# A hybrid decoder trunk on one core: fixed bank for seventeen accumulators, fused value products, one scaling on GpSimd, and two norms' factors through DRAM

## The chip, the cores and the metric

The kernel runs on one core of one Trainium2 chip. The metric is the device time of one execution in microseconds. Before the change it is 1033.41 us, the median of three runs (1032.59 to 1033.46).

A core has engines that run side by side: TensorE (PE: matrix products; its weight loads are listed as PEld), VectorE (DVE), ScalarE (ACT), GpSimd (POOL) and SyncE (SP, which here only issues transfers). Each takes its own instructions in order and waits on semaphores of the others. TensorE writes its sums to eight banks of PSUM, each 128 partitions by 512 float32; a bank is free for the next sum when DVE or ACT has read it.

## The reference, cut to what matters

Two layers over 512 tokens of 1024 channels, in float32. The first is a Conformer convolution module and a SwiGLU feed-forward part. The second takes queries, attends over keys and values that are projected once, and has its own feed-forward part:

```python
def rmsnorm(x, g):
    xf = x.astype(jnp.float32)
    xf = xf * lax.rsqrt(jnp.mean(xf * xf, axis=-1, keepdims=True) + EPS)
    return (xf * g.astype(jnp.float32)).astype(x.dtype)
...
            if l == N_A_LAYERS:
                kv = rmsnorm(h, norm_kv) @ w_kv
                k_flat, v_flat = jnp.split(kv, 2, axis=-1)
...
            q = (rmsnorm(h, norm_mix[l]) @ w_q[j]).reshape(B, S, N_HEADS, HEAD_DIM)
            attn = banded_sink_attention(q, k_shared, v_shared, sinks[j], rel_bias)
            h = h + attn @ w_o[j]
        h = h + swiglu_ffn(rmsnorm(h, norm_ffn[l]), ffn_w_up[l], ffn_w_down[l])
    return rmsnorm(h, norm_final)
```

Keys and values have four heads of 64 channels each, so the value projection is a product of 512 tokens by 1024 channels by 256 columns.

## The kernel before, in words

The activations stay in SBUF with channels on the partitions and the 512 tokens along the free axis. Weights come as 258 chunks of 512 KB (128 partitions by 1024 floats) in the order of `PLAN`; SyncE's queue loads them into six `raw` buffers, nine chunks ahead at most (`load`, L286). Most chunks are then split into a rounded high part `whi` (ACT, L322) and the rest `wlo` (DVE, L325), four buffers of each, since a float32 product is made of three products of parts, high by high, high by low and low by high (`mm3`, L418 to L420). Sums of weight blocks that the seven-product scheme of the feed-forward parts needs are prepared in DRAM: SyncE copies a block (L300), GpSimd's queue adds another to it (L314), and a later load reads it.

An RMS norm's factor is one number for each token. `Rms.add` squares and adds the channels' tiles; `step1` sums over the partitions with matmuls into four columns (L533), makes mean and epsilon on DVE (L535) and the power of -1/2 on GpSimd (L538), so that `rs` holds the factors with tokens on the partitions. To multiply tiles that have tokens along the free axis, the factors must stand in every partition: DVE puts them on the diagonals of four blocks (`diag`, L543; for two blocks it is ACT, L548), a matmul with a matrix of ones spreads them into a bank (`spread`, L562), and ACT copies this to `bc` (L556). The norm is not multiplied into the inputs of the products but into their results, so `bc` is read only when a product is evacuated. Two norms have all four blocks (n == 4): the one of keys, values and queries, whose `step1` and `step2` stand around the projection of the values, and the one of the second feed-forward part.

The keys come first (`kb`, 24 matmuls of 512 columns for each of two halves of the channels). Then the values (`vb`, four banks, one for each 128 tokens): there the tokens are the stationary operand, and for each of 8 channel blocks and 4 token blocks `mm3` streams 256 columns of `whi`, of `wlo` and of `whi` again. DVE scales them to `vq` (L1499). `query(0, 0)` follows, then a change of the PSUM pools: the pool of eight banks (`ps8`) is closed, and a pool of one (`ps1`) and one of seven (`ps7`) are opened in its place, since the later stages keep one bank apart (`last_bank`). Then `query(0, 1)` and the attention run as a pipeline, whose score tiles `sc` (four buffers of 128 by 4 by 257 floats) lie in a pool that was opened before the last down projection of the first layer.

The order within each engine is that of a planner in the language's framework, which simulates the program and places what is ready; `issue_after` in the code holds some instructions behind others. It also chooses which bank of a pool an accumulator gets.

At the end the last product comes in four blocks of 128 tokens and two halves g of the channels. For each block the sum of squares, its power (`power`, GpSimd) and the scaling (`scale`) follow, then the store. `then` keeps the order of these steps on each engine as written. `ends` is the last block, number 3; half 0 of a block is scaled by ACT, half 1 by DVE, and SyncE's queue stores all pieces but one, which goes by ACT's queue.

Of the kernel before, what the change touches and what calls it, by code (L numbers as in the profile page):

```python
# [18 lines left out]
P = 128  # L19
# [26 lines left out]
SEVEN = ("A11 B11", "S1 T1", "S2 T2", "A12 B21", "S3 T3", "S4 B22", "A22 T4")  # L46
LOWS = ((0, 2, 4), (6, 8))
# [170 lines left out]
def hybrid_trunk(ctx: ExitStack, tc: tile.TileContext, xT, W, prm_in, wdw_in, sinks, relb, onehot, fin, lead, out):  # L218
# [14 lines left out]
    room, stay = ExitStack(), ExitStack()  # L233
    ctx.enter_context(room)
    ctx.enter_context(stay)
    psum_at = [room.enter_context(tc.tile_pool(name="ps8", bufs=8, space=PSUM))]
    last_bank, rooms, spare, turn, alone = [], [], [], [0], [0]
# [4 lines left out]
    def bank():  # L242
        if spare:
            spare.append(spare.pop(0))
            return rooms[spare[-1]][:, 0].rearrange("p a s -> p (a s)") if spare[-1] is not None else one_of(last_bank[0])
        turn[0] = (turn[0] + alone[0]) % 8
        return one_of(last_bank[0] if turn[0] == 7 else psum_at[0])
# [85 lines left out]

    def advance():
        u = stream["use"]
        share[1] += share[0]
        for _ in range(2):
            if share[1] >= 1 and not withheld:
                share[1] -= 1
                next(preparing[0], None)  # L340
        load(u + DMA_AHEAD)
        while stream["split"] < min(len(PLAN), u + SPLIT_AHEAD):
            i = stream["split"]
            stream["split"] += 1
            if i in NATIVE:
                splits[i] = (raws.pop(i), None)
                continue
            hi = wpool.tile([P, 1024], F32R, tag="whi", name=uid("whi"))
            lo = wpool.tile([P, 1024], F32R, tag="wlo", name=uid("wlo"))
            splits[i] = (hi, lo)  # L350
            split_weights(hi, lo, raws.pop(i))
# [46 lines left out]
    def get(*key):  # L398
# [11 lines left out]
        return tuple(w and w.rearrange("p (a b) -> p a b", **sh) for w in (hi, lo))  # L410

# [96 lines left out]
    class Rms:  # L508
# [17 lines left out]
        def step1(self):  # L526
# [12 lines left out]
            if self.pinned:  # L539
                biased[0] = mean  # L540
            self.diag = temp()[:, 0:self.w]
            if n == 4:
                nc.vector.tensor_mul(self.diag.rearrange("p (n q) -> p n q", n=n),  # L543
                                     ident.unsqueeze(1).to_broadcast([P, n, P]),
                                     self.rs.unsqueeze(2).to_broadcast([P, n, P]))
            else:
                for i in range(n):
                    self.turned = nc.scalar.mul(self.diag[:, i * P:(i + 1) * P], ident, self.rs[:, i:i + 1]).ins  # L548
# [855 lines left out]

    part2 = ExitStack()
# [57 lines left out]
    if True:  # L1463
# [19 lines left out]
        for half in range(2):  # L1483
            whi, wlo = get("kv", 1, half)
            for k in range(4):
                xh, xl = xkv[half * 4 + k]
                for n in range(4):
                    ts = slice(n * P, (n + 1) * P)
                    mm3(vb[n][:, 0:256], (xh[:, ts], xl[:, ts]), (whi[:, k, :], wlo[:, k, :]),
                        half == 0 and k == 0, half == 1 and k == 3)  # L1490
# [7 lines left out]
        for n in range(4):  # L1498
            nc.vector.tensor_scalar(vq[:, n].rearrange("p a g c -> p (a g c)"), vb[n][:, 0:256], rs[:, n:n + 1], None,  # L1499
                                    op0=ALU.mult)  # L1500
# [24 lines left out]
        def pair(gp, jp, n0):  # L1525
# [9 lines left out]
            for _ in units:  # L1535
                sc = at.tile([P, 4, 1 + BAND], F32, tag="sc", name=uid("sc"), bufs=4)
# [81 lines left out]
        room.close()  # L1618
        last_bank.append(room.enter_context(tc.tile_pool(name="ps1", bufs=1, space=PSUM)))
        psum_at[0] = stay.enter_context(tc.tile_pool(name="ps7", bufs=7, space=PSUM))  # L1620
# [159 lines left out]
    def scale(b, g):  # L1780
# [4 lines left out]
        elif g:  # L1785
            then("v", lambda: nc.vector.tensor_scalar(o, o, last[:, 0:1], None, op0=ALU.mult))
        else:
# [3 lines left out]
    for b in range(NBLK):  # L1791
# [6 lines left out]
        if b == ends:  # L1798
            break
# [20 lines left out]
    scale(ends - 1, 0)  # L1820
# [30 lines left out]
```

## Time and profile before

| | before |
|---|---|
| median of three runs | 1033.41 us |
| the profiled execution | 1033.16 us |
| its span, first to last instruction | 1031.4 us |
| PE busy | 1021.6 us, 99% of the span |
| DVE, ACT, POOL busy | 811.5, 604.1, 403.6 us |
| granted TensorE clock | 0.998 |

The span is 1.8 us shorter than the execution's own time, and the profiled execution lies 0.25 us below the median. The page gives busy time by engine, the chain of work that ended last, groups of instructions by line, and the transfers. In the timelines each row is start, duration, engine, line, operation, names and shapes; what stands in square brackets is how long the engine stood idle before the row and what released it.

### The profile page before, as it was taken

The numbers are of one execution on the slowest core, as the hardware profiler recorded it, in microseconds if no ns is written. First come the engines' busy times: TensorE is split into PE (matmuls) and PEld (weight loads), VectorE is DVE, ScalarE is ACT, GpSimd is POOL, SyncE is SP. The second block draws the span as 40 slices with busy tenths as digits, with TensorE's granted clock in tenths as the row PEclk, the third lists the DMA queues.
The fourth block names the chain that finished last, engine by engine and source line by source line (L and its number), as shares of the span: only waits on it lengthen the run. The fifth ranks groups of instructions, "written<-read, shape, count | busy, mean of one in ns | idle before, by whom it ended". The sixth has DMA issues, their size and how long they took to land.

```text
span 1031.4 us, 16960 instructions
## 1 busy us (share of the span) xinstructions
PE 1021.6 (99%) x6220; PEld 910.6 (88%) x6220; DVE 811.5 (79%) x1250; ACT 604.1 (59%) x1036; POOL 403.6 (39%) x512
## 2 busy tenths in 40 slices
PE   9999999999999999999999999999999999999997
PEld 8888889999989998899888777779988888888985
DVE  3999988897789796387567465769799989878796
ACT  3887796957675553255444365548745555555564
POOL 3999997852121332033335255501314234001113
PEclk9999999999999999999999999999999999999999
DMA  9999837998999999699998996985699897755642
GB/s 355 334 327 266 155 123 213 280 268 221 300 274 307 277 310 311 181 288 332 327 316 261 252 242 188 223 266 161 248 285 288 251 272 214 242 167 182 216 150 83
DMA packets 68240, 256.69 MB, mean 249 GB/s; under 512 B 7835, under 2 KB 14140, under 8 KB 67132
## 3 DMA queue, kind: packets, MB, share of 16 engines
q1 hardware_dynamic: 54044, 204.95, 56.6%
q0 software_dynamic: 13824, 50.34, 26.3%
q8 instruction: 49, 0.80, 0.3%
q10 hardware_dynamic: 288, 0.31, 0.1%
q14 instruction: 35, 0.29, 0.1%
HBM read 250.32 MB, written 105.91 MB: 345 GB/s over the span
## 4 chain that ended last, share of the span: by engine, by line
PE 77%; DVE 5%; issue 1%; POOL 0%; ACT 0%; DVEq 0%; ACTq 0%; POOLq 0%
PE rooms L834 15%; PE bank L418 14%; PE bank L420 14%; PE bank L419 14%; PE rooms L973 9%; PE bank L446 3%; DVE wlo L325 2%; PE bank L1548 1%; PE bank L1590 1%; PE bank L1577 1%; DVE bank L1082 1%; PE rooms L1755 1%; DVE tmp L521 0%; PE bank L1673 0%; PE bank L1755 0%
## 5 line engine op out<-in xcount | busy, mean ns | idle before, releaser
L322 ACT CAST whi<-raw 128x1024 fp32r<-128x1024 f32 x246 | 257.5, 1049 | 289.0 <-PE bank L419 152.3
L325 DVE TENSOR_TENSOR wlo<-raw,whi 128x1024 fp32r<-128x1024 f32 x246 | 328.4, 1341 | 94.8 <-ACT whi L322 94.4
L418 PE MATMUL bank<-quad,whi 128*128 128x256 f32 (+1 forms) x752 | 241.1, 325 | 0.8 <-DVE qs L1519 0.8
L419 PE MATMUL bank<-quad,whi 128*128 128x256 f32 (+1 forms) x752 | 240.7, 322 | 0.0
L420 PE MATMUL bank<-quad,wlo 128*128 128x256 f32 (+1 forms) x752 | 240.0, 322 | 0.1
L1075 POOL TENSOR_TENSOR pr<-pr,pr 128x256 f32<-128x256 f32 x208 | 154.5, 791 | 6.9 <-ACT pr L1074 6.8
L418 PEld LDWEIGHTS bank<-quad,whi 128*128 128x128 f32 x752 | 142.2, 190 | 12.9 <-issue 1.3
L419 PEld LDWEIGHTS bank<-quad,whi 128*128 128x128 f32 x752 | 142.9, 190 | 10.9 <-issue 0.6
L420 PEld LDWEIGHTS bank<-quad,wlo 128*128 128x128 f32 x752 | 142.5, 190 | 11.3 <-issue 0.4
L1082 DVE SCALAR_TENSOR_TENSOR bank<-apad,wdw,bank 128x256 f32<-128x256 f32 x248 | 112.5, 486 | 3.4
L915 POOL TENSOR_TENSOR kept<-kept 128x512 f32<-128x512 f32 x22 | 31.6, 1435 | 207.2 <-ACT kept L912 207.1
L1074 ACT ACTIVATE pr<-apad,wdw 128x256 f32<-128x256 f32 x208 | 98.4, 501 | 14.9 <-POOL pr L1075 13.1
L1033 PE MATMUL bank<-quad,w 128*128 128x256 f32 x448 | 98.7, 380 | 0.0
L1033 PEld LDWEIGHTS bank<-quad,w 128*128 128x128 f32 x448 | 84.9, 190 | 11.8 <-DVE bank L1082 0.2
L973 PE MATMUL rooms<-whi,form 128*128 128x512 f32 x280 | 86.7, 389 | 0.0
L418 PE MATMUL bank<-rows,whi 128*128 128x256 f32 x280 | 78.8, 282 | 0.0
L419 PE MATMUL bank<-rows,whi 128*128 128x256 f32 x280 | 78.8, 282 | 0.0
L420 PE MATMUL bank<-rows,wlo 128*128 128x256 f32 x280 | 78.8, 283 | 0.0
L314 POOL DMA_DIRECT2D sum<-in_W_dram x48 | 44.6, 993 | 63.5 <-DVE wlo L325 54.4
L314 POOL DMA_DIRECT2D sum<-sum x48 | 44.2, 948 | 55.5 <-DVE wlo L325 35.4
L915 POOL TENSOR_TENSOR up<-up 128x512 f32<-128x512 f32 x16 | 30.9, 1930 | 86.9 <-ACT up L912 78.5
L834 PE MATMUL rooms<-rows,whi 128*128 128x512 f32 x256 | 63.3, 392 | 0.0
(274 smaller groups left out, 1887.7 us busy)
## 6 DMA issues: line engine op xcount, KB each, us to landing
raw<-in_W_dram SPq DMA_DIRECT2D x162, 512.0 KB, 6.5
raw<-sum SPq DMA_DIRECT2D x96, 512.0 KB, 4.5
sum<-in_W_dram SPq DMA_DIRECT2D x64, 512.0 KB, 7.9
sum<-in_W_dram POOLq DMA_DIRECT2D x48, 512.0 KB, 8.8
sum<-sum POOLq DMA_DIRECT2D x48, 512.0 KB, 9.1
sum<-in_W_dram SPq DMA_DIRECT2D x4, 4096.0 KB, 34.7
w<-in_W_dram SPq DMA_DIRECT2D x14, 512.0 KB, 8.6
fd<-fs SPq DMA_DIRECT2D x1, 3072.0 KB, 44.0
```

Source lines behind the costliest of these rows:

```text
L314: additions.append(nc.gpsimd.dma_start(summed[c], chunk(c, SUMS[c[2]][1]), accum_op=ALU.add, max_dma_last_dim=4096).ins)
L322: on_act = nc.scalar.copy(hi, src).ins
L325: latest[:] = [on_act, lo_engine[0].tensor_sub(lo, src, f32(hi)).ins]
L418: nc.tensor.matmul(out, w[0], x[0], start=start, stop=False, **kw)
L419: nc.tensor.matmul(out, w[0], x[1], start=False, stop=False, **kw)
L420: stamp[0] = nc.tensor.matmul(out, w[1], x[0], start=False, stop=stop, **kw).ins
L834: stamp[0] = nc.tensor.matmul(to, w[e][:, which, k, :], x, start=opens and not e and k == 0, stop=e == 1 and k == 3, skip_group_check=True ...
L973: stamp[0] = nc.tensor.matmul(out, x, w[:, ws], start=first and u == 0 and e == 0 and j == 0, stop=u == len(self.pairs) - 1 and e == 1 and ...
L1033: mm = nc.tensor.matmul(self.pb[:, w * W2:(w + 1) * W2], w1_of(ct, w, k), x[k] if x else xg[k][:, tok], start=k == 0, stop=k == KT - 1)
L1074: on_act = nc.scalar.mul(pr, a[:, j:j + W2], tap(j))
L1075: on_pool = pool_op(nc.gpsimd.tensor_add(pr, acc, pr))
L1082: on_dve = nc.vector.scalar_tensor_tensor(yt if i == nd - 1 else c, src, tap(i), c if i else self.shift, op0=ALU.mult, op1=ALU.add)
```

## The change

Four edits.

1. **Banks.** The pool of one bank and the pool of seven are opened at the start, and the change of pools after `query(0, 0)` is gone. `bank()` counts its calls, and the seventeen calls whose number stands in `APART` get the single bank.
2. **Values.** The two chunks of the value weights are split in two pieces each, not into `whi` and `wlo` but into tiles of the attention's `sc` shape, high and low part side by side. One matmul of 512 columns then makes high by high and high by low in two halves of a bank, a second one of 256 columns adds low by high. ACT scales the one half to `vq`, DVE scales the other and adds.
3. **Scaling.** Half 0 of block 2 (`ends - 1`) is scaled by GpSimd, right after that block's power, and no longer by ACT after the last block's power; its store is issued at that place too.
4. **Norms.** For the two norms with four blocks `step1` goes on with two transfers on SyncE's queue: `rs` is written to a row of 512 floats in DRAM, and the row is read back into `bc` on all partitions. `diag`, the matmul with ones and ACT's copy are left out for them.

```diff
+APART = (2, 12, 19, 25, 32, 39, 43, 52, 57, 67, 76, 84, 92, 100, 108, 115, 123)
...
-    room, stay = ExitStack(), ExitStack()
-    ctx.enter_context(room)
+    last_bank = [ctx.enter_context(tc.tile_pool(name="ps1", bufs=1, space=PSUM))]
+    stay = ExitStack()
     ctx.enter_context(stay)
-    psum_at = [room.enter_context(tc.tile_pool(name="ps8", bufs=8, space=PSUM))]
-    last_bank, rooms, spare, turn, alone = [], [], [], [0], [0]
+    psum_at = [stay.enter_context(tc.tile_pool(name="ps7", bufs=7, space=PSUM))]
+    rooms, spare, turn, alone, taken = [], [], [0], [0], [0]
...
+        taken[0] += 1
+        if taken[0] in APART:
+            return one_of(last_bank[0])
         turn[0] = (turn[0] + alone[0]) % 8
...
+    def split_side(src):
+        sides = []
+        for k in range(0, 4, 2):
+            both = side_of().rearrange("p (k e) c -> p k e c", e=2)[:, :, :, 0:256]
+            hi, lo = (both[:, :, e].bitcast(F32R) for e in range(2))
+            split_weights(hi, lo, src[:, k:k + 2])
+            sides += [both[:, e].bitcast(F32R) for e in range(2)]
+        return sides
...
+            if PLAN[i][:2] == ("kv", 1):
+                splits[i] = split_side(raws.pop(i).rearrange("p (a b) -> p a b", a=4))
+                continue
...
+            if n == 4:
+                row = dpool.tile([1, S], F32, tag="row", name=uid("row"), bufs=2)
+                nc.sync.dma_start(row.rearrange("a (n p) -> p (a n)", p=P), self.rs)
+                nc.sync.dma_start(self.bc, row.to_broadcast([P, S]))
+                self.stage = 2
+                return mm.ins
             self.diag = temp()[:, 0:self.w]
-            if n == 4:
-                nc.vector.tensor_mul(self.diag.rearrange("p (n q) -> p n q", n=n),
-                                     ident.unsqueeze(1).to_broadcast([P, n, P]),
-                                     self.rs.unsqueeze(2).to_broadcast([P, n, P]))
-            else:
-                for i in range(n):
...
+    def side_of():
+        return at.tile([P, 4, 1 + BAND], F32, tag="sc", name=uid("sc"), bufs=4)
...
-            whi, wlo = get("kv", 1, half)
+            sides = get_sides("kv", 1, half)
...
-                    mm3(vb[n][:, 0:256], (xh[:, ts], xl[:, ts]), (whi[:, k, :], wlo[:, k, :]),
-                        half == 0 and k == 0, half == 1 and k == 3)
+                    nc.tensor.matmul(vb[n], xh[:, ts], sides[k], start=half == 0 and k == 0, stop=False)
+                    stamp[0] = nc.tensor.matmul(vb[n][:, 0:256], xl[:, ts], sides[k][:, 0], start=False,
+                                                stop=half == 1 and k == 3).ins
...
-            nc.vector.tensor_scalar(vq[:, n].rearrange("p a g c -> p (a g c)"), vb[n][:, 0:256], rs[:, n:n + 1], None,
-                                    op0=ALU.mult)
+            v = vq[:, n].rearrange("p a g c -> p (a g c)")
+            nc.scalar.mul(v, vb[n][:, 256:512], rs[:, n:n + 1])
+            nc.vector.scalar_tensor_tensor(v, vb[n][:, 0:256], rs[:, n:n + 1], v, op0=ALU.mult, op1=ALU.add)
...
-        room.close()
-        last_bank.append(room.enter_context(tc.tile_pool(name="ps1", bufs=1, space=PSUM)))
-        psum_at[0] = stay.enter_context(tc.tile_pool(name="ps7", bufs=7, space=PSUM))
...
+        elif b == ends - 1:
+            then("p", lambda: nc.gpsimd.tensor_scalar(o, o, last[:, 0:1], 0.0, op0=ALU.mult, op1=ALU.add))
         else:
             then("s", lambda: nc.scalar.mul(o, o, last[:, 0:1]))
...
         if b == ends:
+            scale(b - 1, 0)
             break
...
     scale(ends - 1, 1)
-    scale(ends - 1, 0)
     scale(ends, 0)
```

`get_sides` is `get` without the reshaping: it runs the same loads, splits and paced background work, and returns the split pieces.

More of the change, by code (lines that the diff above doesn't have):

```diff
@@ L410, in get, with get_sides @@
         return tuple(w and w.rearrange("p (a b) -> p a b", **sh) for w in (hi, lo))
+    def get_sides(*key):
+        advance()
+        pace()
+        due[0] += rate[0]
+        tick(int(due[0]))
+        due[0] -= int(due[0])
+        i = stream["use"]
+        assert PLAN[i] == key
+        stream["use"] += 1
+        return splits.pop(i)
     stamp = [None]
@@ L540, in step1 @@
                 biased[0] = mean
-            self.diag = temp()[:, 0:self.w]
-            if n == 4:
-                nc.vector.tensor_mul(self.diag.rearrange("p (n q) -> p n q", n=n),
-                                     ident.unsqueeze(1).to_broadcast([P, n, P]),
-                                     self.rs.unsqueeze(2).to_broadcast([P, n, P]))
-            else:
-                for i in range(n):
-                    self.turned = nc.scalar.mul(self.diag[:, i * P:(i + 1) * P], ident, self.rs[:, i:i + 1]).ins
+            if n == 4:
[4 more added lines that the diff above has]
+                return mm.ins
+            self.diag = temp()[:, 0:self.w]
+            for i in range(n):
+                self.turned = nc.scalar.mul(self.diag[:, i * P:(i + 1) * P], ident, self.rs[:, i:i + 1]).ins
             return mm.ins
@@ L1535, in pair @@
             for _ in units:
-                sc = at.tile([P, 4, 1 + BAND], F32, tag="sc", name=uid("sc"), bufs=4)
+                sc = side_of()
                 nc.gpsimd.tensor_copy(sc[:, :, 0].rearrange("p (g e) -> p g e", g=2), sinks4)
```

## The prediction, made before the changed kernel was run

> **What bounds the kernel now.** I read the page's busy times first, then the list of waits on PE and on SyncE's queue, then the timelines around the places that the change touches.
>
> ```profile
> span 1031.4 us, 16960 instructions
> PE 1021.6 (99%) x6220; PEld 910.6 (88%) x6220; DVE 811.5 (79%) x1250; ACT 604.1 (59%) x1036; POOL 403.6 (39%) x512
> ...
> PE bank L495 <- POOL ones_m L492: 1.0, 1, 1.0
> PE bank L418 <- DVE qs L1519: 0.8, 1, 0.8
> PE bank L1021 <- DVE quad L993: 0.3, 1, 0.3
> ...
> SPq L286 <- DVE wlo L325: 655.7, 227, 14.1
> ```
>
> PE stands still for 9.8 us of the span, most of it before its first and after its last matmul; its waits for others come to 2.1 us, and one of them, 0.8 us at L418, lies in the middle. SyncE's loads wait for the split of an older chunk (L325), so the weights come as fast as PE uses them up. PE sets the end: a matmul that goes shortens the kernel by its step, and a microsecond on another engine is worth nothing until PE waits for it.
>
> **The values.** The timeline of PE in the second part of the value projection, and the evacuations behind the first query:
>
> ```profile
> 558.92 0.28 PE L418 MATMUL bank<-whi,quad 128*128 128x256 f32 x1
> 559.04 1.02 PE L562 MATMUL bank<-tmp,ones_m 128*128 128x512 f32 x2
> 559.49 0.68 PE L419 MATMUL bank<-wlo,quad 128*128 128x256 f32 x1
> 560.01 0.28 PE L420 MATMUL bank<-whi,quad 128*128 128x256 f32 x1
> ...
> 565.40 0.28 PE L420 MATMUL bank<-whi,quad 128*128 128x256 f32 x1
> 565.52 0.40 PE L418 MATMUL bank<-quad,whi 128*128 128x512 f32 x1
> ...
> 576.20 0.39 PE L420 MATMUL bank<-quad,wlo 128*128 128x512 f32 x1
> 577.38 0.50 PE L418 MATMUL bank<-quad,whi 128*128 128x512 f32 x1 [0.78 <-DVE qs L1519]
> ...
> L418 PE MATMUL bank<-whi,quad 128*128 128x256 f32 x32 | 9.1, 286 | 0.0
> ```
>
> A row's duration overlaps the next row's, so a matmul costs the distance of two starts: the 45 steps from 560.01 to 565.40 make 0.120 us for 256 columns, and the 47 steps of the first query's 48 matmuls, from 565.52 to 576.20, make 0.227 us for 512. There are 32 groups of three matmuls (32 on each of the three lines). A group goes from 3 x 0.120 = 0.360 to 0.227 + 0.120 = 0.347, and 32 x 0.0135 give **0.43 us less**. This needs a 512-column stream over two rows of 256 that stand 257 floats apart to run like a plain one, for which no row stands; if it ran no faster than two of 256 the gain would be 0, and nothing in the rows gives more than 0.43. I take 0.43. Around it, the split becomes two pieces of half the size on ACT and DVE, and the evacuation gets an ACT multiplication beside each of four DVE ones. The last value product is over when the first query starts at 565.52, and `vq` is first read in the attention, behind the second query (its scores are the row of L1548 below), so a microsecond or two there costs nothing; the `sc` tiles that hold the pieces are free again at the same point.
>
> **The spreads by matmul.** At 559.04 the spread's matmuls (L562, two rows) stand between two value products. Without them L420 would start two steps of 0.120 behind 558.92, at 559.16; it starts at 560.01: 0.85 us. The second norm:
>
> ```profile
> 721.64 1.02 PE L562 MATMUL bank<-tmp,ones_m 128*128 128x512 f32 x2
> 722.49 0.60 PE L1673 MATMUL bank<-ident,h 128*128 128x128 f32 x4
> ...
> 728.10 0.68 DVE L911 TENSOR_TENSOR kept<-kept,rsbc 128x512 f32<-128x512 f32 x1
> ```
>
> 722.49 - 721.64 is again 0.85. Both go: **1.70 us less**. The diagonals on DVE and the copy on ACT go with them, where they are covered now by PE.
>
> **The pools.** After 576.20 the next start would be 576.43; it is 577.38, just behind DVE's second evacuation of the first query (576.63, below). That query(0, 1) waits for query(0, 0)'s evacuation is what closing a pool of eight asks: its successors start when all of its tiles are released. Without the change of pools the new sums take any free bank. So **0.95 us less**, with 0 as the other end, if another cause stands behind this wait. Before that point the single bank only fixes for seventeen calls what the planner chose among eight; PE waits for no bank there now, and I count it as nothing (it would cost what one such wait costs, 0.8 us, if an old sum stood in a bank too long).
>
> **The transfers in place of the first spread.** What surrounds it now, from the timelines of POOL, SyncE, DVE and PE:
>
> ```profile
> 555.93 1.95 POOL L538 TENSOR_TENSOR rs<-ms,mhalf 128x4 f32<-128x4 f32 x1 [4.89 <-DVE ms L535]
> 557.39 1.13 SPq L300 DMA_DIRECT2D sum<-in_W_dram  x2
> 561.49 0.33 SPq L286 DMA_DIRECT2D raw<-in_W_dram  x1
> 561.38 1.28 DVE L1495 TENSOR_TENSOR kq<-bank,rsbc 128x512 f32<-128x512 f32 x2
> 576.63 0.69 DVE L1519 SCALAR_TENSOR_TENSOR qs<-bank,rsbc 128x512 f32<-128x512 f32 x1 [2.03 <-PE bank L420]
> 583.05 1.58 PE L1548 MATMUL bank<-kq,qs 64*128 64x128 f32 x16
> 587.27 2.76 POOL L1567 TENSOR_SCALAR sc<-sc,sm 128x128 f32<-128x128 f32 x5 [16.77 <-DVE sm L1565]
> ```
>
> The transfers in that stretch (552 to 575); then, of the whole run, the read from a DRAM table, with the least, median and most of its time to landing, and the stores:
>
> ```profile
> sum<-in_W_dram SPq DMA_DIRECT2D x6, 512.0 KB, 8.8
> sum<-sum POOLq DMA_DIRECT2D x4, 512.0 KB, 17.3
> ...
> bias<-fd SPq DMA_DIRECT2D x8, 256.0 KB, 9.4
> ...
> DMA to landing us min/median/max: 3.2/9.4/9.9
> ...
> out_dram<-room SPq DMA_DIRECT2D x7, 256.0 KB, 2.1
> ```
>
> `rs` is ready at 557.9. The write (2 KB in 512 pieces) stands on SyncE's queue behind two copies of 512 KB issued from 557.39 on; the read (256 KB) is issued only when it has landed. Early bound: 2.1 and 2.1 like an undisturbed store, `bc` at 562. Late bound: the write like a copy, 8.8, the read like the slowest `bias`, 9.9, `bc` at 576.6. The middle is nearest to the row of the copies, since the write waits behind two of them: 557.9 + 8.8, then 3.2 for a read with SyncE's own queue empty behind it: 570.
>
> Who waits? DVE's evacuation of the keys (L1495), 561.4 now, would stand until 570, and behind it the values' evacuation, a split, and the two `qs`. PE comes to `query(0, 1)` at 576.43 - 0.43 - 0.85 = 575.15. Seven banks are then taken: two of keys, three of the values (the fourth is in the single bank), two of the first query; the first that comes free is a key bank, half of 1.28, 0.64 us behind `bc`. So `bc` may be as late as 574.5 and costs nothing; at 570 there are 4.5 us left. At the late bound PE waits 576.6 + 0.64 - 575.15 = 2.1 us. Queued behind on SyncE: the load that now goes at 561.49 would go at about 567, and so would a copy behind it that GpSimd adds to; GpSimd's next work for the attention comes at 587.27, so there is room. I count **0 us**, with 0 to 2.1 for the range.
>
> A page of the Trainium skill speaks against this step. It says (DMA: Bandwidth & Descriptors, section Specifications) that pieces under 512 bytes make the engine read, modify and write; the write's pieces have 4 bytes. No run so far shows such a transfer; by the page the write lies at the slow end and the sum loses the 2.1 us of the late bound, by the rows above it loses nothing.
>
> **The transfers in place of the second spread.** Rows of POOL, SyncE and ACT:
>
> ```profile
> 710.79 1.95 POOL L538 TENSOR_TENSOR rs<-ms,mhalf 128x4 f32<-128x4 f32 x1 [42.81 <-DVE ms L535]
> 713.00 0.32 SPq L286 DMA_DIRECT2D raw<-sum  x1
> 725.87 1.05 ACT L322 CAST whi<-raw 128x1024 fp32r<-128x1024 f32 x1 [1.76 <-PE bank L419]
> ```
>
> Here `rs` is ready at 712.7 and `bc` first read at 728.1 (L911): 15.4 us for two transfers, 12 by the same middle (8.8 + 3.2). SyncE stands still until the write has landed, up to 721.5, and the load that goes at 713.00 waits with all behind it. That load's chunk (counted from the first, the cast at 725.87 is its own) would land by 721.5 + 8.8 = 730.3 at worst, 4.4 us too late for the cast; but the cast is made three chunks ahead of PE, 3 x 24 x 0.120 = 8.6 us, less some 2.4 for cast and split. PE does not wait: 0.
>
> **The scaling.** The last rows of POOL, DVE's and ACT's scalings and the last store, and the kind of GpSimd instruction that is added:
>
> ```profile
> 1022.59 1.30 POOL L1775 TENSOR_TENSOR room<-room,gain 128x512 f32<-128x512 f32 x1 [0.68 <-PE rooms L1755]
> 1023.85 0.54 POOL L1770 TENSOR_TENSOR rs<-ss,mhalf 128x1 f32<-128x1 f32 x1
> 1025.45 0.55 POOL L1770 TENSOR_TENSOR rs<-ss,mhalf 128x1 f32<-128x1 f32 x1 [1.05 <-DVE ss L1817]
> ...
> 1025.02 0.71 ACT L1788 ACTIVATE room<-room,rs 128x512 f32<-128x512 f32 x1
> 1026.03 0.72 ACT L1788 ACTIVATE room<-room,rs 128x512 f32<-128x512 f32 x1 [0.30 <-POOL rs L1770]
> 1026.78 0.39 ACTq L1789 DMA_DIRECT2D out_dram<-room  x1
> ...
> L1567 POOL TENSOR_SCALAR sc<-sc,sm 128x256 f32<-128x256 f32 x48 | 22.1, 475 | 7.1 <-DVE sm L1565 6.8
> ```
>
> GpSimd is free from 1024.39 to 1025.45. 256 columns took 475 ns, so 512 should take up to 950: done at 1025.34, 0.39 us ahead of ACT's end now, 1025.73. ACT's last scaling waits for the power and not for ACT, so it starts no earlier. What can gain is the store of 256 KB that leaves 0.39 us sooner, ahead of the others, of which ACT's, the last, leaves at 1026.78. Bounds: all of 0.39 at the end, or, if the scaling took 1.30 us like the weighing before it (L1775), the last power and all behind it come 0.24 us later. I take **0.2 us less**.
>
> **The sum.** 0.43 + 1.70 + 0.95 + 0.2 = 3.28 us. The profiled execution took 1033.16 us (span and 1.8 around it): 1029.9; the median of the runs lies 0.25 above it: **1030.1 us**. By the bounds of these terms: 1029.9 with the whole 0.39 at the end; 1030.5 without the values' gain, 1031.1 without the pools'.
>
> **The rivals.** *Factors late by some microseconds*: `bc` at the late bound, PE stands 2.1 us before the second query, 1032.2. For it: transfers of 8 to 10 us in that stretch; against it: 4.5 us of room. *SyncE's chain becomes the bound, slower*: the read takes as long as GpSimd's own additions just then, 17.3 (they share the engines): 557.9 + 8.8 + 17.3 = 584.0, and PE, with all seven banks taken, waits 584.0 + 0.64 - 575.15 = 9.5 us: 1039.6. It decides from `bc` at 574.5 on, microsecond for microsecond, and the kernel is slower than before once `bc` comes after 577.8. Against it: SyncE's own transfers beside those additions took 8.8. *The planner's new order gives some back*: all from the key projection on is planned anew, and a displaced evacuation costs what the pool's wait cost, 0.8 to 1 us; with one or two of them 1031 to 1032. *The change of pools was not the cause* of the wait at 577.38: 1031.1, still faster.
>
> **How the numbers follow.** A difference of 0.2%, 2.1 us, is about what a measurement of this kernel can tell. The forecast, with small misses of its terms and the pools' case, has 63% (1029.5 to 1031.2, all faster by over 2.1); late factors 13% (1031.2 to 1033.5) and the new order 11% (mostly within 2.1 us of before, a tenth of it faster); the slower chain 13%, from 1035.5 up. That makes 0.64 faster, 0.23 the same, 0.13 slower. The range of 1028.9 to 1033.9 leaves out the slower chain and a little of the rest.
>
> **What would show it.** Right: no L562 row of 512 columns in the two places, PE's starts at the values 0.227 and 0.120 apart, no gap before the second query, L1495 starting between 562 and 574, stores of block 2 that leave before 1025.4 on the old clock, and a span near 1028.1. Wrong: a PE row that waits for L1495, L1519 or L1499 between the values and the first scores, casts that wait for a DMA around 720, or PE waits in the attention that were not there.

## The result: slower by 17 microseconds

| | before | after |
|---|---|---|
| median of four runs each | 1033.0 us | 1050.42 us (1049.66 to 1052.84) |
| ratio, 95% interval | | 1.0169 (1.0157 to 1.0181) |
| the profiled execution, its span | 1033.16, 1031.4 us | 1052.84, 1051.1 us |
| PE busy | 1021.6 us, 99% | 1023.2 us, 97% |

The forecast was 1030.1 us, with a range up to 1033.9. The sign was wrong. In the changed kernel a line stands further down, by 4 at the loads and splits, by 27 from the matmuls to the norms and by 28 to 33 beyond: a load's L286 is L290, a matmul's L418 to L420 are L445 to L447, L1495 (`kq`) is L1527; the new write and read are L570 and L571, the new value matmuls L1520 and L1521.

The page's head and the waits of PE, of the kernel after (waits: total, times, longest):

```profile
span 1051.1 us, 16902 instructions
PE 1023.2 (97%) x6184; PEld 910.9 (87%) x6184; DVE 811.1 (77%) x1250; ACT 603.7 (57%) x1039; POOL 406.1 (39%) x513
...
PE bank L445 <- DVE kq L1527: 15.0, 1, 15.0
PE bank L445 <- DVE kept L905: 2.5, 1, 2.5
PE bank L445 <- DVE kept L899: 1.7, 1, 1.7
```

There are 36 matmuls fewer, and three waits that were not there. The old one for `qs` is gone. The first wait belongs to the first norm, the other two to the second.

**The first norm.** Timelines of POOL, SyncE, DVE and PE of the kernel after:

```profile
555.68 1.95 POOL L565 TENSOR_TENSOR rs<-ms,mhalf 128x4 f32<-128x4 f32 x1 [4.88 <-DVE ms L562]
...
557.66 0.38 SPq L570 DMA_DIRECT2D row<-rs  x1
558.14 0.45 SPq L290 DMA_DIRECT2D raw<-in_W_dram  x1
581.08 0.33 SPq L571 DMA_DIRECT2D rsbc<-row  x1
...
589.69 1.29 DVE L1527 TENSOR_TENSOR kq<-bank,rsbc 128x512 f32<-128x512 f32 x2 [32.96 <-DMA rsbc<-row]
...
575.03 0.39 PE L447 MATMUL bank<-quad,wlo 128*128 128x512 f32 x1
590.44 0.80 PE L445 MATMUL bank<-quad,whi 128*128 128x512 f32 x1 [15.02 <-DVE kq L1527]
```

The write leaves at 557.66, 23.4 us before the read may go. The prediction had it behind two copies on SyncE's queue; now a copy goes 4.4 us ahead of it (553.29), and a load and the other copy go right behind it, at 558.14 and 558.64. The read lands 8.6 us later (the transfers of this stretch):

```profile
rsbc<-row SPq DMA_DIRECT2D x1, 256.0 KB, 8.6
row<-rs SPq DMA_DIRECT2D x1, 2.0 KB, 23.4
```

PE has made its seven banks full at 575.03 and stands until half of `kq` is done. The next start would have been 575.26: 15.18 us. Then it comes back slowly: the eight steps from 590.44 to 593.90 take 3.46 us where eight of 0.227 make 1.82, 1.64 us more. The windows of PE (busy time and instructions, granted clock, DMA share, GB/s) show why:

```profile
590.00:594.00 4.00, 3.56 (x9) 0.53 0.00 0
...
754.00:757.50 3.50, 3.50 (x19) 0.53 1.03 430
```

After the pause the clock is granted at about half (0.53 from 590 to 594); the last row belongs to the second norm, below.

**The second norm.** Timelines of SyncE, ACT and PE, and the throughput in 40 slices of 725 to 750 us:

```profile
727.37 0.37 SPq L570 DMA_DIRECT2D row<-rs  x1
727.85 0.48 SPq L290 DMA_DIRECT2D raw<-sum  x1
738.46 0.32 SPq L571 DMA_DIRECT2D rsbc<-row  x1
...
745.11 1.05 ACT L326 CAST whi<-raw 128x1024 fp32r<-128x1024 f32 x1 [5.67 <-DMA raw<-sum]
750.18 1.05 ACT L326 CAST whi<-raw 128x1024 fp32r<-128x1024 f32 x1 [4.03 <-DMA raw<-in_W_dram]
...
748.16 0.36 PE L445 MATMUL bank<-rows,whi 128*128 128x256 f32 x1 [1.73 <-DVE kept L899]
753.74 0.39 PE L445 MATMUL bank<-rows,whi 128*128 128x256 f32 x1 [2.48 <-DVE kept L905]
...
GB/s 184 393 131 33 0 3 92 13 0 0 0 0 72 20 20 13 7 20 7 0 33 13 7 39 210 197 177 282 288 262 243 285 197 147 200 275 377 406 511 688
```

The write takes 11.1 us here. A slice of the last row is 0.625 us: from the fourth slice (726.9) to the 24th (740) none reaches 100 GB/s, all queues together, although a load of 512 KB has been issued at 727.85. (The first two of these slices lie before the write's packets, which start at 728.3.) That load's cast waits for it until 745.11, and the next cast waits until 750.18 for a load that could be issued only behind the read. The evacuations on ACT and DVE behind each of the two casts come late, and PE waits for their banks, 1.9 and 2.6 us by its steps (0.120 each). It loses another 1.6 to the clock, which is granted at 0.53 from 754.0 to 757.5.

The account of the profiled run: 15.18 + 1.64 + 1.9 + 2.6 + 1.6 = 22.9 us lost. The span grew by 19.7, so the rest of the change gained 3.2; this figure is what the account leaves over, and was not measured by itself. (This run is the slowest of the four; the medians lie 17.4 apart.)

### The profile page after: what moved, and what is told of

The parts are those of the page before. It is cut to its first block, busy times and chain, and to the rows that moved or that the text cites. A ratio compares the mean times of both kernels' runs of the same rounds, so it can differ in the third digit from the quotient of the medians.

```text
span 1051.1 us, 16902 instructions
## 1 busy us (share of the span) xinstructions
PE 1023.2 (97%) x6184; PEld 910.9 (87%) x6184; DVE 811.1 (77%) x1250; ACT 603.7 (57%) x1039; POOL 406.1 (39%) x513
## 4 chain that ended last, share of the span: by engine, by line
PE 64%; DMA 7%; issue 6%; DVE 5%; POOL 1%; ACT 1%; SPq 0%; ACTq 0%; POOLq 0%; DVEq 0%
PE rooms L862 15%; PE bank L445 11%; PE bank L447 11%; PE bank L446 11%; PE rooms L1001 9%; DMA row<-rs 3%; PE bank L473 3%; DVE wlo L329 2%; DMA sum<-sum 1%; DMA raw<-in_W_dram 1%; DVE bank L1110 1%; PE bank L1581 1%; DMA rsbc<-row 1%; PE bank L1610 1%; PE rooms L1785 1%
## 5 line engine op out<-in xcount | busy, mean ns | idle before, releaser
L445 PE MATMUL bank<-quad,whi 128*128 128x256 f32 (+1 forms) x752 | 242.1, 326 | 15.0 <-DVE kq L1527 15.0
L447 PE MATMUL bank<-quad,wlo 128*128 128x256 f32 (+1 forms) x752 | 240.5, 323 | 0.1
L445 PEld LDWEIGHTS bank<-quad,whi 128*128 128x128 f32 x752 | 142.5, 191 | 27.4 <-DVE kq L1527 15.4
L447 PEld LDWEIGHTS bank<-quad,wlo 128*128 128x128 f32 x752 | 142.9, 191 | 11.3 <-issue 0.4
L445 PE MATMUL bank<-rows,whi 128*128 128x256 f32 x280 | 79.9, 286 | 4.2 <-DVE kept L905 2.5
L447 PE MATMUL bank<-rows,wlo 128*128 128x256 f32 x280 | 79.5, 285 | 0.0
```

The source lines that it names most:

```text
L445: nc.tensor.matmul(out, w[0], x[0], start=start, stop=False, **kw)
L447: stamp[0] = nc.tensor.matmul(out, w[1], x[0], start=False, stop=stop, **kw).ins
```

## The experiments

Twelve kernels ran. "Before" lay between 1033.0 and 1033.6 us beside them. Diffs are against the kernel after unless another is named.

### Only the transfers undone

```diff
-            if n == 4:
+            if False:
                 row = dpool.tile([1, S], F32, tag="row", name=uid("row"), bufs=2)
...
+            if n == 4:
+                nc.vector.tensor_mul(self.diag.rearrange("p (n q) -> p n q", n=n),
+                                     ident.unsqueeze(1).to_broadcast([P, n, P]),
+                                     self.rs.unsqueeze(2).to_broadcast([P, n, P]))
```

> The changed kernel with the spread by diagonal and matmul put back for both norms; banks, values and scaling stay changed. Theory 'the row's write': all of the loss lies in the two norms' transfers, and the other edits keep what the changed kernel's own rows show of them: some 0.2 us from the values, 0.95 from the pools, 0.27 from the end, about 1031.5 us against 1033.0. Rival 'the other edits cost too' (planner's order, banks): 1033.5 or more, with waits of PE that were not there before.

Measured: 1031.38 us (1030.61 to 1032.96), ratio 0.9984 (0.9975 to 0.9993). The waits of PE:

```profile
...
PE bank L1054 <- DVE quad L1026: 0.8, 2, 0.6
```

The wait of the change of pools is gone, none has come in the middle. The waits that are left, this one and 1.0 us for `ones_m`, lie in the first 10 us. Banks, values and scaling together are worth 1.9 us; the loss is all in the transfers.

### One norm at a time

```diff
-            if n == 4:
+            if n == 4 and self.eng is nc.gpsimd:
...
+            if n == 4:
+                nc.vector.tensor_mul(self.diag.rearrange("p (n q) -> p n q", n=n),
```

That is the first norm alone through DRAM; with `nc.vector` in the condition it is the second alone.

> As the changed kernel, but the second norm is spread by matmul again; only the first goes through DRAM. Theory 'the row's write': the first write lands after 20 to 24 us, PE waits about 15 us before the second query and 1.6 us more at a lower clock: 1031.5 - 0.85 + 16.8 = 1047.4. Rival 'the two waits are one' (the second comes from the first's upset of the queues): the same time here as with both, about 1050.

> As the changed kernel, but the first norm is spread by matmul again; only the second goes through DRAM. Theory 'the row's write': its write holds up the loads by about 10 us and PE waits 4 to 4.5 us around the first gates: 1031.5 - 0.85 + 4.5 = 1035.2. Rival 'the two waits are one': no wait, 1030.7.

Measured: the first alone 1046.06 us (ratio 1.0123, 1.0105 to 1.0141), the second alone 1036.56 (1.0035, 1.0022 to 1.0049). Against the 1031.38 without transfers that is +14.7 and +5.2, together 19.9, and both at once cost 19.0: within 0.9 us the two losses add up. The transfers and the wait of the first alone, then the waits of the second alone:

```profile
rsbc<-row SPq DMA_DIRECT2D x1, 256.0 KB, 9.9
row<-rs SPq DMA_DIRECT2D x1, 2.0 KB, 18.9
...
PE bank L445 <- DVE kq L1532: 11.9, 1, 11.9
```

```profile
PE bank L445 <- DVE kept L910: 2.4, 1, 2.4
...
PE bank L445 <- DVE kept L904: 0.8, 1, 0.8
```

### Is it the pieces, or the place in the queue?

The same row in four pieces of 512 bytes, after a transposing matmul and a copy by ACT:

```diff
...
+                pt = bank()
+                nc.tensor.transpose(pt[0:4, 0:P], self.rs, ident)
+                four = small.tile([4, P], F32, tag="four", name=uid("four"), bufs=2)
+                nc.scalar.copy(four, pt[0:4, 0:P])
+                nc.sync.dma_start(row.rearrange("a (n p) -> (a n) p", p=P), four)
```

> As the changed kernel, but the factors are transposed by one matmul of 128 columns first (at the place where the spread stood) and copied by ACT, so that the row is written in 4 pieces of 512 bytes, not 512 of 4 bytes. Theory 'pieces': the write then lands in 3 to 9 us like any other small transfer, and the factors stand at 572 to 578: 1030.2 to 1033. Rival 'place in the queue' (any write there waits for GpSimd's additions, whatever its pieces): the first write still takes 20 us or more, PE waits 15 us or more, 1045 to 1050.

Measured: 1031.86 us (1029.77 to 1036.74), ratio 0.9990 (0.9976 to 1.0004). SyncE's issues and PE's waits:

```profile
559.57 0.28 SPq L586 DMA_DIRECT2D row<-four  x1
565.87 0.35 SPq L587 DMA_DIRECT2D rsbc<-row  x1
...
PE bank L445 <- DVE kept L910: 1.0, 1, 1.0
...
PE bank L445 <- DVE kq L1532: 0.3, 1, 0.3
```

With the same bytes, and with the same five of GpSimd's additions beside it, the write takes 6.3 us in place of 23.4 (and 4.7 in place of 11.1 at the second norm). The place in the queue is not the cause; the pieces are. (SyncE's load and copy went 2.8 and 2.5 us ahead of this write and not behind it; the next version has them in the changed kernel's order.) What is left are two small waits and the transposing matmul.

The second way to fewer pieces is 128 of 16 bytes, each partition's four factors side by side. This kernel leaves out putting the factors back into the tokens' order, so that its products take the factors of other tokens; it is for the times alone:

```diff
-                nc.sync.dma_start(row.rearrange("a (n p) -> p (a n)", p=P), self.rs)
+                nc.sync.dma_start(row.rearrange("a (p n) -> p (a n)", p=P), self.rs)
```

> As the changed kernel, but the row is written as 128 pieces of 16 bytes, four factors of a partition side by side; the factors then stand in another order in the row, so the two norms' products are scaled with the factors of other tokens. Theory 'each piece has its price' (some 20 ns each, 512 pieces 10 us, and all other traffic stands): 2.6 us for the pieces, the writes land 4 to 9 us after their issue, PE waits at most 3 us: 1030 to 1034. Rival 'any write under 512 bytes stops the traffic for about 10 us', whatever the count: writes of 10 us and over as with 512 pieces, 1047 to 1050.

Measured: 1030.38 us (1029.72 to 1032.35), ratio 0.9971 (0.9959 to 0.9983). The first write took 6.8 us and its read 11.7, the second 2.6 and 8.1:

```profile
558.36 0.33 SPq L570 DMA_DIRECT2D row<-rs  x1
565.17 0.33 SPq L571 DMA_DIRECT2D rsbc<-row  x1
...
PE bank L445 <- DVE kq L1527: 1.5, 1, 1.5
```

The profiled execution is the slowest of the six, 1032.35, the only one over 1030.5; no trace shows whether its wait of 1.5 us stood in the others. Their 1030.3 is close to the 1030.1 that the prediction had said of the whole change.

### Does the neighbourhood make the first write slow?

The first write takes twice the second. Beside it stand five of GpSimd's adding transfers, beside the second two. I tried to hold the five back:

```diff
+        withheld.append(True)
         rms.step1()
...
         flush()
+        withheld.clear()
```

> As the changed kernel, but GpSimd's additions are held back from before the first norm's sums until the values are done, so that none of the five that were issued beside the first write is. Theory 'each piece has its price': the first write still takes about 10 us, the factors stand near 575, PE waits 0 to 4 us there and 4.5 at the second norm: 1034 to 1038. Rival 'turns' (each piece waits for a packet of an addition on its DMA engine, that is all): the first write lands in 3 to 4 us, no wait before the second query, 1033 to 1035.

Measured: 1050.92 us, ratio 1.0167 (1.0152 to 1.0182); the write took 20.0 us. It says nothing: five additions still came between 559 and 562, since they had been handed to the planner earlier. Whether the additions are what doubles the first write's time stays open; that the first write is the slower one also with 16-byte pieces (6.8 against 2.6) and with four (6.3 against 4.7) only fits it.

### The disputed cost by itself

This is the kernel without transfers, with unread writes on ScalarE's queue in the last down projection, one behind the other. `few` are the second norm's 512 factors on 128 partitions. In order: 512 pieces of 4 bytes into SBUF, then into DRAM 128 of 16 bytes, 512 of 4, the same 512 bytes apart, and 128 of 64 bytes:

```diff
...
+            nc.scalar.dma_start(spread_out[:, :, 0], few)
...
+            nc.scalar.dma_start(r16.rearrange("a (p n) -> p (a n)", p=P), few)
...
+            nc.scalar.dma_start(r4.rearrange("a (n p) -> p (a n)", p=P), few)
...
+            nc.scalar.dma_start(apart.rearrange("(n p) c -> p n c", p=P)[:, :, 0], few)
...
+            nc.scalar.dma_start(r64, ident[:, 0:16])
```

> The kernel with both spreads by matmul (as in the run without the transfers), with five writes that nobody reads, on ScalarE's queue, some 5.5 us or more apart in the last down projection, where few transfers are under way: the 512 factors in pieces of 4 bytes to another SBUF tile; in 128 pieces of 16 bytes to DRAM; in 512 pieces of 4 bytes to a row in DRAM; in 512 pieces of 4 bytes that stand 512 bytes apart in DRAM; and 128 pieces of 64 bytes to DRAM. Theory 'each piece into DRAM has its price': about 2 to 3 us in SBUF, 4 to 5 for 128 pieces, 10 to 12 for 512 in a row. If the price is that of neighbours in one line of memory, the 512 pieces that stand apart land in 3 to 5 us; if it is that of each piece, in 10 to 12 as well. Rival 'turns': all five land in 2 to 4 us here, since there is little to take turns with.

The time of the one run was 1034.18 us. The transfers of two stretches (977 to 987, 986 to 1001), and the throughput in 40 slices of the second:

```profile
probe<-rs ACTq DMA_DIRECT2D x1, 2.0 KB, 3.8
r<-rs ACTq DMA_DIRECT2D x1, 2.0 KB, 1.4
...
r<-rs ACTq DMA_DIRECT2D x1, 2.0 KB, 10.8
apart<-rs ACTq DMA_DIRECT2D x1, 2.0 KB, 7.2
...
GB/s 98 76 0 164 448 393 448 404 415 350 25 3 0 0 0 0 0 0 0 0 11 55 109 44 44 66 44 33 0 44 11 33 22 55 33 55 11 197 218 218
```

The same 2 KB take 1.4 us in 128 pieces of 16 bytes (128 of 64 bytes also took 1.4) and 10.8 in 512 pieces of 4, and 512 pieces of 4 into SBUF take 3.8. While the slow write runs (from 989.1 on, the ninth slice), the throughput goes from over 400 GB/s to nothing, and stays under 110 until it has landed at 999.8. It is not that nothing was there to move: the four loads of 512 KB issued in this stretch took 9.8 us (median). So the price is there without the norm, without GpSimd's additions and on another queue.

I then varied the number and the size apart, in the same way, all into DRAM: 512 pieces of 16 bytes, 128 of 4, 512 of 4 that lie 512 bytes apart, 512 of 8:

```diff
...
+            nc.scalar.dma_start(r16.rearrange("a (n p c) -> p (a n) c", p=P, n=4), ident[:, 0:16].rearrange("p (n c) -> p n c", n=4))
...
+            nc.scalar.dma_start(r1.rearrange("a p -> p a"), few[:, 0:1])
...
+            nc.scalar.dma_start(apart.rearrange("(n p) c -> p n c", p=P)[:, :, 0], few)
...
+            nc.scalar.dma_start(r8.rearrange("a (n p c) -> p (a n) c", p=P, n=4), ident[:, 0:8].rearrange("p (n c) -> p n c", n=4))
```

> e1_no_transfers plus four further unread writes on ScalarE's queue in the last down projection, each behind the one before and all into DRAM: 512 pieces of 16 bytes, 128 pieces of 4 bytes, 512 pieces of 4 bytes put 512 bytes apart, 512 pieces of 8 bytes. Of e7_probes stand 10.75 us for 512 adjacent pieces of 4 bytes, 7.2 for 512 of them 512 bytes apart, 1.41 for 128 pieces of 16 bytes. Theory 'so much for each small piece': all three of 512 pieces take 7 to 11 us and the 128 of 4 bytes a quarter of that, 2 to 3 us. Rival 'pieces of 4 bytes alone': 512 of 16 bytes and 512 of 8 bytes take about as long as the 512 into SBUF (3.8 us or less), the 128 of 4 bytes 2 to 3 us. Rival 'neighbours': pieces that lie side by side in one stretch of DRAM are slow, and those 512 bytes apart take under 5 us when nothing is beside them. The time of the whole is that of e1 or up to 5 us over it; it carries nothing.

The time of the one run was 1031.84 us. The transfers of the four (stretches 976 to 982, 982 to 990, 998 to 1003):

```profile
r<-ident ACTq DMA_DIRECT2D x1, 8.0 KB, 5.1
...
raw<-in_W_dram SPq DMA_DIRECT2D x2, 512.0 KB, 9.9
raw<-sum SPq DMA_DIRECT2D x1, 512.0 KB, 9.6
r<-rs ACTq DMA_DIRECT2D x1, 0.5 KB, 7.9
apart<-rs ACTq DMA_DIRECT2D x1, 2.0 KB, 7.6
...
r<-ident ACTq DMA_DIRECT2D x1, 4.0 KB, 3.6
```

512 pieces of 16 bytes take 5.1 us and 512 of 8 bytes 3.6; but 128 pieces of 4 bytes, a quarter of the number, take 7.9, and the loads beside them 9.6 to 9.9. The first two theories had 2 to 3 us for these. The same loads in the same stretch (982 to 990) of the kernel without transfers:

```profile
raw<-in_W_dram SPq DMA_DIRECT2D x2, 512.0 KB, 3.9
raw<-sum SPq DMA_DIRECT2D x1, 512.0 KB, 3.3
```

By these times alone it would be the size of the piece, 4 bytes into DRAM, more than the number. The packets show more. A transfer is moved in packets, here one for each piece and a few signals, and the profile says when each passed. The first two rows are the 512 adjacent pieces of the earlier probes (989.9 to 990.4, then to 999.8), the next two the 128 pieces (983.2 to 984.2, then to 989.9), the last the 512 that lie 512 bytes apart in the earlier probes (1003.5 to 1006.7):

```profile
DMA packets 530, 0.00 MB, mean 4 GB/s; under 512 B 530, under 2 KB 530, under 8 KB 530
DMA packets 61, 0.25 MB, mean 27 GB/s; under 512 B 0, under 2 KB 0, under 8 KB 61
...
DMA packets 191, 0.13 MB, mean 128 GB/s; under 512 B 160, under 2 KB 160, under 8 KB 191
DMA packets 49, 0.20 MB, mean 35 GB/s; under 512 B 0, under 2 KB 0, under 8 KB 49
...
DMA packets 714, 0.65 MB, mean 202 GB/s; under 512 B 557, under 2 KB 557, under 8 KB 714
```

The adjacent pieces have all passed at 990.4, half a microsecond after the first, and the write lands 9.4 us later; the 128 pieces have passed at 984.2 and land 5.8 us later. In between no small packet follows, and all queues together move 27 and 35 GB/s. The time lies behind the pieces and not in them, so a quarter of the number saves little. The second norm's write shows the same: its packets pass from 728.2 to 728.7, and it lands at 738.5.

The pieces that lie apart behave otherwise. They stood right behind a slow write both times, and their first packets came 3.7 and 5.7 us after their issue, more than half of their 7.2 and 7.6 us. They passed over 3.0 and 1.4 us and landed some 0.5 us behind the last, and the whole traffic ran at 340 GB/s ahead of them (999.9 to 1003.5) and at 343 beside them (993.2 to 994.7). What the traces show to be slow is pieces of 4 bytes side by side in DRAM: the rival "neighbours" fits, and neither "so much for each small piece" nor "pieces of 4 bytes alone" does. Its own forecast, under 5 us with nothing beside it, was not put to the test, and no run wrote a norm's row with its pieces apart. That the adjacent pieces also passed more densely is not ruled out as the cause. The 8- and 16-byte probes were read from another tile (a constant one), which may matter too.

### Versions that keep the transfer

The second norm alone in four pieces, its step three products earlier, the first norm by a matmul:

```diff
...
-        if n == 8:
+        if n == 5:
```

> The first norm by matmul again, the second by the transposing matmul and 4 pieces of 512 bytes, with its step three products earlier than in the run with four pieces. If the transfers there cost PE nothing: 0.7 us less than the run without transfers, 1030.7. If SyncE's stand between its write and its read makes the loads late all the same: PE waits about 1 us as in the run with four pieces, 1031.5 to 1032.

Measured: 1031.41 us (1030.18 to 1031.87), ratio 0.9979 (0.9971 to 0.9988), with no wait at the norm. The median equals that of the kernel without transfers, although the trace shows a gain at the norm: from PE's first `rows` product of the second feed-forward part to its first product into `rooms` it takes 25.73 us, against 26.49 without transfers. The profiled execution gives this back where the two kernels' edits are alike, 0.3 us before the norm and 0.4 behind the last matmul. Other kernels differ there by as much, so a gain of 0.76 us can't be told from the time.

The second norm alone, then both, in 128 pieces of 16 bytes, read back in that order and put right by the products that use them, which read the factors with a stride:

```diff
...
-                nc.vector.tensor_mul(gate, gate, rs_bc)
+            by_token = self.rows.rms.step2().rearrange("p (q n) -> p n q", n=4)
...
+                    four = gate.rearrange("p s (a q) -> p (s a) q", a=2)
+                    nc.vector.tensor_mul(four, four, by_token)
```

> e1_no_transfers with the second norm's factors alone through DRAM, written as 128 pieces of 16 bytes (each partition's four factors side by side), read back in that order, the gates taking the factors with a stride, so that every token has its own factor. By e4_pieces128 the write takes 2.6 us and the read 8.1, and PE waits for nothing at this norm: e1's 1031.4 less the two short matmuls' 0.85 us, about 1030.5. Rival: the planner's order without the first norm's transfers lets the loads come late as in e3_second_only, and a wait of 1 to 2 us takes the gain: 1031.4 to 1032.5.

> Both norms' factors through DRAM as 128 pieces of 16 bytes, read back in that order and taken with a stride, every token with its own factor. Theory 'it was the number of pieces': as e4_pieces128, the first write about 7 us, its read about 12, a wait of about 1.5 us ahead of the second query, none at the second norm: 1030.4, some 0.3% under the kernel before. Rival: the first norm's read is the limit whatever the pieces, and its wait takes all that the matmul cost: 0.65 us or more over e11_second_16.

Measured: 1032.39 us (ratio 0.9991, 0.9983 to 1.0000) and 1032.68 (1.0002, 0.9989 to 1.0015; 1030.65 to 1038.51). PE waits at neither norm, so the transfers are hidden; the gain went elsewhere. The gates' products on VectorE (16 of them; busy, mean ns) in the kernel without transfers:

```profile
L944 DVE TENSOR_TENSOR kept<-kept,rsbc 128x512 f32<-128x512 f32 x16 | 12.0, 752 | 0.8 <-ACT kept L918 0.8
```

and in the version with the second norm alone, with PE's wait at the start of the down projection:

```profile
L947 DVE TENSOR_TENSOR kept<-kept,rsbc 128x512 f32<-128x512 f32 x16 | 20.7, 1294 | 0.4 <-ACT kept L918 0.4
...
PE rooms L1011 <- DVE wlo L329: 0.6, 1, 0.6
```

The strided read costs 8.7 us of VectorE, and PE, at its first matmuls of the down projection (860 us), waits 0.6 us for a remainder that VectorE makes (1.1 with both norms). The 0.85 us of the two short matmuls are gained at the norm (25.64 against 26.49 us for the stretch named above) and given back 130 us later. The rest of the 1.0 us to the kernel without transfers lies, in the profiled executions, before the norm and behind the last matmul (0.4 each), where the edits are alike. Two of the versions with the first norm through DRAM scatter widely: twelve runs with both norms in order span 7.9 us and ten with four pieces 7.0, against 2.4 of ten without transfers; no trace shows why. Lastly the same version, with one copy by ACT that puts the factors in order:

```diff
+                if self.eng is nc.vector and self.w == 4 * P and self.ordered is None:
+                    self.ordered = new_bc()
+                    nc.scalar.copy(self.ordered.rearrange("p (n q) -> p n q", n=4), self.bc.rearrange("p (q n) -> p n q", n=4))
```

> e11_second_16, with the factors put into the tokens' order once by ScalarE (one copy of 128 x 512 read with a stride, after the read from DRAM has landed), so that the 16 gates' products take them side by side as in e1_no_transfers. Theory 'the strided products were what e11 lost': in e11 each of the 16 took 1.29 us of VectorE in place of 0.75, 8.7 us in all, and PE waited 0.6 us for the remainder of a weight at the start of the down projection; with the one copy they take 0.75 again, that wait is gone and the two short matmuls' 0.85 us remain as gain: 1030.4 to 1030.8. Rival: the write and the read themselves cost as much as the matmuls (the copy stands where the copy out of PSUM stood, the loads start some 0.4 us later): the time of e1, 1031.4, or of e11, 1032.4.

Measured: 1033.96 us (1032.43 to 1034.99), ratio 1.0002 (0.9993 to 1.0011). The products took 752 ns again and the wait at 860 was gone, as the theory said, but ACT's timeline and PE's waits show a new one:

```profile
722.53 1.14 ACT L590 COPY rsbc<-rsbc 128x512 f32<-128x512 f32 x1 [6.07 <-DMA rsbc<-row]
...
PE bank L445 <- DVE kept L908: 2.0, 1, 2.0
```

The copy stands on ACT from 716.5 on, and waits 6.07 us for the transfer; in the version before, ACT made two casts in that time (718.1 and 721.3). PE waits 2.0 us for what came late behind the copy, and its clock is granted at 0.79 from 727 to 735; the norm's stretch takes 29.35 us. Neither theory had that.

## Why the prediction was wrong

**The step that failed** is "The transfers in place of the first spread": its late bound gave the write the 8.8 us of a 512 KB copy. No row of before held a write in 4-byte pieces, and I bounded it from above by a row of large pieces, as if bytes and company in the queue set the time. It took 23.4 us, and 10.8 beside SyncE's loads alone. The read was inside its bounds (8.6 us, with 9.9 at most allowed), but the middle's 3.2 was too little: at this norm no version's read took less than 8.6, and the longest took 11.7. So the factors came at 589.7, not at 570, and the 0 us became 16.8.

**The limit of that step was right.** It said that `bc` may come as late as 574.5, and that each microsecond beyond costs PE one. By it 589.69 makes 589.69 + 0.64 - 575.15 = 15.18 us, and 15.18 were measured; that the hundredths agree is chance, since PE's next start was 575.26 and its late one 0.11 behind half of `kq`. The other versions bear it out, each by its own next start, which lies up to 1.5 us later than 575.15 (`kq` starting, and PE's loss by its steps): 574.66 (0.1) with both norms in 16-byte pieces, 575.09 (0.5) with four pieces, 576.91 (1.7) with 16-byte pieces out of order, 587.09 (12.1) with the first norm alone. What I had not counted is the slow clock behind the pause, 1.64 us.

**The second norm** failed by the same price. The step had the chain right, and named its sign ("casts that wait for a DMA around 720"): with a write of 8.8 the load would have landed 4.4 us late for its cast, inside the reserve. But the load did not stand still behind the write; it had gone 0.48 us after it, and crawled while the write ran, 17.2 us to its landing. What stood was the queue behind the read, and so a second cast came late as well. The 0 became 6.1 us.

**The rivals.** "SyncE's chain becomes the bound, slower" had the place, the limit and the sign (1039.6), at 13%; it laid the delay to the read beside GpSimd's additions, and it was the write. "Factors late by some microseconds" is nearest to what the four pieces made of it (waits of 0.3 and 1.0 us; that their 1031.9 lies near its 1032.2 is chance). The sentence drawn from the Trainium skill (DMA: Bandwidth & Descriptors, section Specifications) pointed the right way: pieces far under 512 bytes were the trouble (side by side, as the probes have it). I let it cost no more than the late bound of the rows, 2.1 us; the runs bear its direction out, though not 512 bytes as the edge, since 128 pieces of 16 bytes took 1.4 us alone, and at the norms (5.5 and 6.8 at the first, 2.3 to 2.9 at the second) about as long as four pieces of 512 bytes or less (6.3; 4.4 and 4.7).

**The gains were right in sum**, 3.28 us forecast and 3.2 left over in the account above, but not term by term:

- Spreads: 1.70 forecast. The two rows are gone; in the version with the second norm alone in 16-byte pieces the stretch around that norm is 0.85 us shorter, as said. For the first norm no run shows the gain by itself.
- Pools: 0.95 forecast; the wait is gone in the kernel without transfers. The pools weren't put back alone, so that they were its cause fits, and is not shown.
- Values: 0.43 forecast, about 0.2 measured. A group takes some 0.355 us in place of 0.360: a 512-column matmul over the two halves steps by 0.236 in the mean (0.229 to 0.243), not 0.227.
- Scaling: 0.2 forecast; from the last matmul's start to the end 7.67 us became 7.40, but kernels with the same end lie between 7.13 and 7.57, so it can't be told from 0.1 or 0.5. GpSimd's scaling took 0.70 us, under the bound of 0.95.

Without the transfers 0.95 + 0.43 + 0.2 = 1.58 of the forecast remain, and 1.9 were measured.

## What to carry to other kernels

Cost a transfer by the size and the place of its pieces, not by its bytes; where no row shows such pieces, the price is open upward, and one unread write in a quiet place measures the least of it (10.8 us here, against 23.4 at the norm). A chain of two transfers stands in for a 0.85 us matmul only if its latest landing is safe: the forecast should have weighed 1.7 us of gain against a limit that 4.5 us of delay would break. And a wait for a DMA costs what is queued behind it on its engine, be it SyncE, ACT or VectorE.

## What the runs showed of the hardware that I had not expected

- Writes of 4-byte pieces side by side in DRAM took 7.9 us (128) and 10.8 (512) away from the norms, 9.3 to 11.1 and 18.9 to 23.4 at them. Away from the norms 512 pieces of 8 bytes took 3.6 us, and pieces of 16 bytes 1.4 (128) and 5.1 (512). Away from the norms and at the second one, the 4-byte packets passed within a microsecond and the landing came 5.8 to 9.8 us behind them; 512 pieces of 4 bytes that lie 512 bytes apart landed 0.5 us behind their last packet.
- Such a write slows the whole core's transfers: under 110 GB/s where 400 ran before, and 512 KB loads of 3.3 to 3.9 us took 9.6 to 9.9.
- After 15 us without a matmul the granted clock was 0.53 over the next four microseconds, which cost PE 1.64 us. The Trainium skill (TensorE: Matmul & The Clock Gate, section "Part 1: The HAM clock gate") has half the clock after an idle window of some 3.4 us, and full clock again after as long a busy one. The first norm agrees; at the second, two pauses of 1.9 and 2.6 us, each shorter than that window, cost as much.
- VectorE's product of 128 x 512 took 1.29 us with one operand read at a stride of four floats, 0.75 without.
